# Two edits in a decoder-block kernel: weight casts and transposes held in another order ahead of the up projection, and the squares of x summed on VectorE instead of GpSimd

## The chip, the cores and the metric

The kernel runs on one core of one Trainium2 chip. The metric is the device time of one execution in microseconds (us), the median over the runs. The engines are TensorE (PE; its weight loads are listed apart as PEld), VectorE (DVE), ScalarE (ACT), GpSimd (POOL) and SyncE (SP); the last one here only issues DMAs.

## The reference, cut to what matters

One decoder layer over 512 tokens and 1024 features, in float32:

```
h  = RMSNorm(x) * g1
q, k, v, u_pool, u_gate = split(h @ w_in)
a  = differential attention(q, k, v)          8 heads, causal
p  = causal pooling with windows 2, 4, 8, 16, then w_pool
x1 = x + (sigmoid(g_A) * a + sigmoid(g_P) * p) @ w_out
h2 = RMSNorm(x1) * g2
x2 = x1 + relu(h2 @ w_up)^2 @ w_down
out = RMSNorm(x2) * gf
```

RMSNorm divides each token's row by the root of the mean of its squares. So the first norm needs the sum over all 1024 features of x squared, and the second needs the finished rows of x1.

## The kernel before

**Products.** Every large matrix is split in two reduced-precision float32 parts, hi (a rounded copy, made by ScalarE) and lo (the rest, a subtraction on VectorE, line 113). A product is three matmuls per tile: hi by hi, hi by lo and lo by hi. The tile of one matmul is 128 rows deep and 512 or 256 columns wide. Weights come from HBM through a few rotating raw buffers, are split, and their buffers are handed on when the last reader has finished.

**Order.** The program text gives each instruction its rank. A planner then fixes, before the run and from a time model of its own, the order of the instructions on each engine; at run time an engine works through its list and waits at the first instruction whose data are missing. The helper `after(later, earlier)` adds only an order between two instructions of one engine. Buffers of equal tag share memory: a tile waits until the tile before it under that tag has been read for the last time.

**The first stage** (lines 179 to 267). x arrives transposed, as eight tiles of 128 features by 512 tokens (`xprep`, line 179). For each of them ScalarE makes the hi part (line 184), VectorE the lo part (line 185), and ScalarE squares it (`xsquare`, line 190). In between come the splits of the weights of v (lines 112 and 113) and of the first q (`wq0`). TensorE starts at once on the first half of v and on q of head 0: 96 matmuls of lines 235 to 237 and 24 of `q0_step`. The squares of tile 0 go straight into the tile `ssx`; those of tiles 1 to 7 go into two alternating buffers, and GpSimd adds each one to `ssx` (line 197). When all are in, two small products with ones on TensorE (`pr`, line 251, and `pc`, line 256) add up the 128 rows, and `rsqrt` (line 200) makes from them the scales `rb` and `rcol`. `pr` and `pc` lie in two of the PSUM banks that the second half of v needs, and a third one is free only when the first half of v has been scaled with `rcol`; so three of the four accumulations of that half wait for this chain. Beside it VectorE works through a chain of small operations for the rotary angles (lines 287 to 321), which ends in a Sine on ScalarE (line 322), with a table load ahead of it and one behind it (line 323).

**The passage to the up projection** (lines 605 to 661). The output projection is computed in two halves of 512 features. The second half goes tile by tile over four tiles t of 128 tokens (line 625), each with eight k steps of three matmuls, of which the steps 6 and 7 need the last of four weight splits. Behind each tile: the sum with x (`x1_add`, line 587), the squares (line 561), the row scale (`row_scale`, lines 568 to 576: three small operations on ScalarE, two on VectorE), the scaled row tile h2 (line 636) and eight transposes on TensorE (line 644), whose results ScalarE and VectorE turn into the operands of the up projection (`forms_h2`, line 590). The up and down projections use a seven-product scheme over 2 by 2 blocks: the operands are the blocks A11, A12, A22 and the sums S1 to S4 (line 533). For the first quarter of the up projection (q = 0) the order is A11, A12, S1, S2, S3, A22, S4. A11 needs only token tiles 0 and 1. A12 and all after it need tiles 2 and 3 as well; S1 needs the parts that line 603 makes of tile 3. A product has four blocks (i, p) of twelve matmuls 256 wide.

**What holds the order there.** Tile t's first matmul stands behind the end of tile t-1 for every t from 1 (line 630). The transposes of tiles 0 and 1 stand behind the matmuls of tiles 1 and 2 (lines 631 to 633). In `up`, the transposes of tile 2 stand behind block (0,1) of A11 and those of tile 3 behind block (0,1) of A12 (lines 785 to 790). The weight casts for A11 (called b11) and A12 (called b21), two each, have no hold: they run as soon as a buffer is free. Those of S1 stand behind the row scale of tile 3 (line 729). The weights of S2 are made in place: when the splits of S1 have read their raw buffer, GpSimd issues a DMA that adds a further block to it (line 685).

Of the kernel before, what the change touches and what calls it, by code (L numbers as in the profile page):

```python
# [51 lines left out]
def block_kernel(ctx, tc, xT, x_tok, gains, pos, consts, w_in, w_v, w_pool, w_out, w_up, w_dn, out):  # L52
# [34 lines left out]
    def tmp(tag, name, shape=(P, S), dt=F32, bufs=2):  # L87
        return tp.tile(list(shape), dt, tag=tag, name=name, bufs=bufs)
# [82 lines left out]


    ssx = tmp("y", "ssx", bufs=1)
    vh = B16(2, F32R, "vh")
    vl = B16(3, F32R, "vl")
    rcol = cf.tile([P, NT, 2], F32, name="rcol")
# [12 lines left out]

    def xsquare(k):  # L190
        xt = gt0[:, k % 4, :]
        if k == 0:
            ins = A.activation(out=ssx, in_=xt, func=AF.Square)
        else:
            sq = tmp("sq", f"sq{k}")
            ins = A.activation(out=sq, in_=xt, func=AF.Square)
            G.tensor_tensor(out=ssx, in0=ssx, in1=sq, op=ALU.add)
        return ins

    def rsqrt(dst, src, t, n):  # L200

# [15 lines left out]
    for n in range(2):  # L217
        accs = [bank((0, 1, 2, 3, 4, 5, 6, 0)[4 * n + t], f"v{n}_{t}") for t in range(NT)]
        for kk in range(4):
            if n == 0:  # L220
                xprep(2 * kk)
            if n == 0 and kk == 0:
                raw, hi, lo = wv0
                nc.sync.dma_start(out=raw[:, 512:], in_=w_v[0, 0, :, 512:])
            else:
                raw, hi, lo = load_w(w_v[n, kk], f"v{n}_{kk}", 2 if n == 0 else 1)
            for k2 in range(2):
                if n == 0 and k2 == 1:
                    xprep(2 * kk + 1)
                sl = slice(k2 * 512, k2 * 512 + 512)  # L230
                split = split_w(raw, hi, lo, sl, eng=V)
                k = 2 * kk + k2
                for t in range(NT):
                    tsl = slice(t * P, t * P + P)
                    T.matmul(accs[t], lhsT=xh[:, k, tsl], rhs=hi[:, sl], start=k == 0, stop=False)
                    T.matmul(accs[t], lhsT=xh[:, k, tsl], rhs=lo[:, sl], start=False, stop=False)
                    T.matmul(accs[t], lhsT=xl[k][:, tsl], rhs=hi[:, sl], start=False, stop=k == NK - 1)
                if n == 0:
                    after(xsquare(k), split)
                    if k > 3:  # L240
                        q0_step(k - 4)
            if n == 0 and kk == 1:
                wq0 = load_w(w_in[0], "q0", 2)
            if n == 0 and 0 < kk < 3:
                i = kk - 1
                split_w(*wq0, slice(i * 512, i * 512 + 512), eng=V)
        if n == 0:
            for k in range(4, NK):
                q0_step(k)
            pr = bank(4, "pr")  # L250
            T.matmul(pr, lhsT=ones, rhs=ssx, start=True, stop=True)
            rsqrt(rb, pr, tmp("sq", "nt1"), D)
            A.mul(out=rb, in_=rb, mul=-0.5)
            pc = bank(5, "pc")
            for t in range(NT):
                T.matmul(pc[:, 2 * t : 2 * t + 2], lhsT=ssx[:, t * P : t * P + P], rhs=ones[:, 0:2], start=True, stop=True)
            rct = cf.tile([P, NT, 2], F32, name="rct")
            rsqrt(rcol, pc[:, 0:8].rearrange("p (a b) -> p a b", a=NT), rct, D)
            A.mul(out=rcol, in_=rcol, mul=-0.5)
        for t in range(NT):  # L260
            vd = [v_[:, 4 * n : 4 * n + 4, t * P : t * P + P] for v_ in (vh, f(vh), vl)]
            av = accs[t].rearrange("p (h d) -> p h d", h=4)
            A.activation(out=vd[0], in_=av, func=AF.Copy, scale=rcol[:, t, 0:1])
            V.scalar_tensor_tensor(
                out=vd[2], in0=av, scalar=rcol[:, t, 0:1], in1=vd[1],
                op0=ALU.mult, op1=ALU.subtract,
            )
# [357 lines left out]
    for t in range(NT):  # L625
        a_ = bank(4 + t, f"po1_{t}")
        for k in range(NK):
            m, end = mm_rows(a_, t, k, ws[k // 2], k == 0, k == NK - 1)
            if t and k == 0:
                after(m, state["po"])  # L630
        if 0 < t < 3:
            for b in range(2):
                after(state["h2T", t - 1, b], end)
        state["po"] = end
        x1_add(t, 1, a_)
        V.scalar_tensor_tensor(out=h2[:, t % 2], in0=x1[:, t, :], scalar=row_scale(t, 1), in1=g2b, op0=ALU.mult, op1=ALU.mult)
        pv = []
        for b in range(2):
            pt = bank((t % 2) * 2 + b, f"h2T{t}_{b}")
            for j in range(4):  # L640
                k = 4 * b + j
                if j == 1:
                    state["h2T", t, b] = state["h2T"]
                state["h2T"] = T.transpose(out=pt[:, j * P : j * P + P], in_=h2[:, t % 2, k * P : k * P + P], identity=ident)
            pv.append(pt.rearrange("p (j q) -> p j q", q=P))
        sl = slice((t % 2) * P, (t % 2) * P + P)
        if t > 1:

            A.copy(out=hw[:, 1, :, sl], in_=pv[0])
            V.tensor_tensor(out=hw[:, 0, :, sl], in0=pv[1], in1=hw[:, 1, :, sl], op=ALU.subtract)  # L650
            forms_h2((S1, S2), sl)
        if t == 3:
            forms_h2((S3,), slice(0, HS))
        for b in range(t // 2, 2):
            hi, lo = (gab[b][:, t // 2, i, :, sl] for i in range(2))
            A.copy(out=hi, in_=pv[b])
            part = V.tensor_tensor(out=lo, in0=pv[b], in1=f(hi), op=ALU.subtract)
            if t == 3:
                after(part, state[S3])
            if t < 2:  # L660
                A.copy(out=h2f[:, b, :, sl], in_=pv[b])
# [8 lines left out]
    def weights(src, q, nm, order):  # L670
# [16 lines left out]
        def parts(rs, b, hold=None, add=None):  # L687

            third = nparts[0] % 3 == 2
            nparts[0] += 1  # L690
            out_ = []
            for c in range(2):
                hi, lo = (
                    (bk if third else wp).tile([P, 1024], F32R, tag=t_ + "b" * third, name=f"{t_}_{nm}{b}_{q}_{c}", bufs=2 if third else 4)
                    for t_ in ("wh", "wl")
                )
                if add is None:
                    cast = split_w(rs[c], hi, lo, eng=V)
                else:

                    cast = A.copy(out=hi, in_=rs[c])
                    A.mul(out=lo, in_=f(hi), mul=-1.0)
                    G.dma_start(out=lo, in_=src[q, add, c], accum_op=ALU.add)
                if hold:
                    after(cast, hold)
                out_.append((hi, lo))
            return out_
# [52 lines left out]
    def up(q):  # L760
# [3 lines left out]
        def product(form, name, onto=None):  # L764
# [3 lines left out]
            for i in range(2):  # L768
                hi, lo = w[i]
                for p in range(2):  # L770
                    begin = None
                    a_ = pa[i][:, p * HS : p * HS + HS]
                    for k in range(4):
                        c = slice((p * 4 + k) * P, (p * 4 + k) * P + P)
                        m = T.matmul(a_, lhsT=hi[:, c], rhs=rh[:, k, :], start=p + k == 0 and onto is None, stop=False, skip_group_check=True)  # L775
                        first[-1] = first[-1] or m
                        begin = begin or m
                        T.matmul(a_, lhsT=hi[:, c], rhs=rl[:, k, :], start=False, stop=False, skip_group_check=True)  # L778
                    for k in range(4):
                        c = slice((p * 4 + k) * P, (p * 4 + k) * P + P)  # L780
                        m = T.matmul(a_, lhsT=lo[:, c], rhs=rh[:, k, :], start=False, stop=k == 3, skip_group_check=True)  # L781
                        if q == 0 and form == A12 and (i, p, k) == (1, 0, 0):
                            after(m, state["h2T"])
                    if q == 0:
                        if (form, i, p) == (A11, 0, 1):
                            for b in range(2):
                                after(state["h2T", 2, b], m)
                        elif (form, i, p) == (A12, 0, 1):
                            for b in range(2):
                                after(state["h2T", 3, b], m)  # L790
                        if form != A11 or i + p:
                            after(begin, state["um"])
                        state["um"] = m
# [226 lines left out]
```

## Time and profile before

| | |
|---|---|
| median of 3 runs | 676.74 us (676.6 to 678.25) |
| the profiled execution | 677.01 us, with a span of 675.1 us in the profile |
| TensorE busy | 664.3 us, 98% of the span |
| VectorE, ScalarE, GpSimd busy | 529.7, 461.6 and 122.3 us |
| granted TensorE clock, mean | 0.997 of full speed |

The difference between the profiled execution's time and its span, 1.9 us, lies outside the first and last instruction. A row of the timeline has start, duration, engine, line, operation, the tile written and the tiles read, the shape and a count if equal neighbours are merged; in brackets stands how long the engine had been idle and what released it. TensorE's matmuls overlap: a 512-wide one is listed with 0.39 us but the next one starts 0.227 us later, a 256-wide one with 0.28 and 0.12 us. So a stall is read from the starts.

### The profile page before, as it was taken

The numbers are of one execution on the slowest core, as the hardware profiler recorded it, in microseconds if no ns is written. First come the engines' busy times: TensorE is split into PE (matmuls) and PEld (weight loads), VectorE is DVE, ScalarE is ACT, GpSimd is POOL, SyncE is SP. The second block draws the span as 40 slices with busy tenths as digits, with TensorE's granted clock in tenths as the row PEclk, the third lists the DMA queues.
The fourth block names the chain that finished last, engine by engine and source line by source line (L and its number), as shares of the span: only waits on it lengthen the run. The fifth ranks groups of instructions, "written<-read, shape, count | busy, mean of one in ns | idle before, by whom it ended". The sixth has DMA issues, their size and how long they took to land.

```text
span 675.1 us, 9993 instructions
## 1 busy us (share of the span) xinstructions
PE 664.3 (98%) x3686; PEld 579.5 (86%) x3686; DVE 529.7 (78%) x879; ACT 461.6 (68%) x741; POOL 122.3 (18%) x137
## 2 busy tenths in 40 slices
PE   9999999999999999999999999999999999999995
PEld 7788888888888888888789988899889998899884
DVE  6955877799979986975578998657994599747995
ACT  8464587978887698883577875367743696356874
POOL 6201110132133212520202020202103021210120
PEclk9999999999999999999999999999999999999998
DMA  7526464335254364574964697776959579493863
GB/s 274 188 69 184 126 152 125 102 94 126 86 141 107 98 169 96 127 192 175 306 197 84 198 218 187 167 191 142 234 183 195 195 155 259 129 212 130 214 125 124
DMA packets 32880, 109.34 MB, mean 162 GB/s; under 512 B 4032, under 2 KB 4928, under 8 KB 32832
## 3 DMA queue, kind: packets, MB, share of 16 engines
q0 software_dynamic: 10656, 38.80, 32.2%
q1 hardware_dynamic: 21744, 69.38, 29.1%
q8 instruction: 29, 0.48, 0.3%
q10 hardware_dynamic: 432, 0.52, 0.2%
q14 instruction: 19, 0.16, 0.1%
HBM read 106.59 MB, written 2.10 MB: 161 GB/s over the span
## 4 chain that ended last, share of the span: by engine, by line
PE 95%; DVE 2%; issue 1%; DMA 1%; ACT 1%; SPq 0%; DVEq 0%
PE um L778 8%; PE um L775 8%; PE um L781 8%; PE dm L865 7%; PE dm L867 7%; PE dm L868 7%; PE o L417 2%; PE ga L132 2%; PE ga L131 2%; PE gp L135 2%; PE k L132 2%; PE gp L132 2%; PE k L131 2%; PE gp L131 2%; PE k L135 2%; PE ga L135 2%
## 5 line engine op out<-in xcount | busy, mean ns | idle before, releaser
L778 PE MATMUL um<-gss,wh_ut 128*128 128x256 f32 x192 | 48.2, 284 | 1.3 <-DVE gss L603 1.3
L867 PE MATMUL dm<-wh_dt,z 128*128 128x512 f32 (+1 forms) x128 | 49.5, 386 | 0.0
L868 PE MATMUL dm<-wl_dt,z 128*128 128x512 f32 (+1 forms) x128 | 49.4, 386 | 0.0
L865 PE MATMUL dm<-wh_dt,z 128*128 128x512 f32 (+1 forms) x128 | 49.3, 387 | 0.0
L775 PE MATMUL um<-gss,wh_ut 128*128 128x256 f32 x192 | 48.2, 283 | 0.0
L883 DVE TENSOR_TENSOR x<-x,dm 128x512 f32<-128x512 f32 x48 | 32.7, 682 | 18.3 <-PE dm L868 18.2
L400 ACT ACTIVATE p<-p,st 128x128 f32<-128x128 f32 (+3 forms) x64 | 35.7, 559 | 14.1 <-DVE st L396 13.8
L685 POOL DMA_DIRECT2D wga_dNone<-w_dn x16 | 14.2, 885 | 154.5 <-DVE wl_dt L113 154.5
L112 ACT CAST wh_ut<-wga_uNone 128x1024 fp32r<-128x1024 f32 x24 | 24.7, 1050 | 25.1 <-PE dm L867 19.5
L112 ACT CAST wh_ub<-wr_u 128x1024 fp32r<-128x1024 f32 x24 | 25.1, 1049 | 22.6 <-PE um L778 13.5
L778 PEld LDWEIGHTS um<-gss,wh_ut 128*128 128x128 f32 x192 | 36.9, 192 | 1.5 <-DVE gss L603 1.5
L867 PE MATMUL dm<-wh_db,z 128*128 128x512 f32 x96 | 37.2, 389 | 0.0
L868 PE MATMUL dm<-wl_db,z 128*128 128x512 f32 x96 | 37.2, 389 | 0.0
L685 POOL DMA_DIRECT2D wga_uNone<-w_up x18 | 15.6, 864 | 117.8 <-DVE wl_ut L113 93.2
L775 PEld LDWEIGHTS um<-gss,wh_ut 128*128 128x128 f32 x192 | 36.9, 192 | 0.0
L865 PE MATMUL dm<-wh_db,z 128*128 128x512 f32 x96 | 35.9, 389 | 0.0
L113 DVE TENSOR_TENSOR wl_ub<-wr_u,wh_ub 128x1024 fp32r<-128x1024 f32 x24 | 29.2, 1220 | 8.4 <-ACT wh_ub L112 8.3
L113 DVE TENSOR_TENSOR wl_ut<-wga_uNone,wh_ut 128x1024 fp32r<-128x1024 f32 x24 | 28.7, 1221 | 8.1 <-ACT wh_ut L112 8.0
L750 DVE TENSOR_TENSOR z<-rawz,z 128x1024 fp32r<-128x1024 f32 x28 | 33.6, 1219 | 1.3 <-ACT z L747 1.3
L747 ACT CAST z<-rawz 128x1024 fp32r<-128x1024 f32 x28 | 28.6, 1045 | 7.0 <-PE dm L868 3.2
L396 DVE CUSTOM_DVE_ANT_0 p<-s,mask 128x128 f32<-128x128 f32 (+3 forms) x64 | 30.3, 484 | 3.4 <-PE s L395 3.3
L112 ACT CAST wh_dt<-wga_dNone 128x1024 fp32r<-128x1024 f32 x24 | 24.9, 1049 | 11.8 <-issue 5.1
(324 smaller groups left out, 2221.1 us busy)
## 6 DMA issues: line engine op xcount, KB each, us to landing
wr_u<-w_up SPq DMA_DIRECT2D x24, 512.0 KB, 5.4
wr_d<-w_dn SPq DMA_DIRECT2D x24, 512.0 KB, 4.3
wga_uNone<-w_up POOLq DMA_DIRECT2D x18, 512.0 KB, 6.7
wga_dNone<-w_dn POOLq DMA_DIRECT2D x16, 512.0 KB, 5.5
wr_k<-w_in SPq DMA_DIRECT2D x8, 512.0 KB, 3.3
wr_ga<-w_in SPq DMA_DIRECT2D x8, 512.0 KB, 3.3
wr_gp<-w_in SPq DMA_DIRECT2D x8, 512.0 KB, 4.0
wl_ga<-w_in POOLq DMA_DIRECT2D x8, 512.0 KB, 5.4
```

The costliest lines, as they stand in the source:

```text
L112: ins = A.copy(out=hi[:, sl], in_=raw[:, sl])
L113: (eng or G).tensor_tensor(out=lo[:, sl], in0=raw[:, sl], in1=f(hi)[:, sl], op=ALU.subtract)
L131: T.matmul(acc, lhsT=hi[:, c], rhs=rh[:, k, :], start=k == 0, stop=False)
L132: T.matmul(acc, lhsT=hi[:, c], rhs=rl[k], start=False, stop=False)
L135: T.matmul(acc, lhsT=lo[:, c], rhs=rh[:, k, :], start=False, stop=k == NK - 1)
L400: A.activation(out=pr[:, c, :N], in_=pr[:, c, :N], func=AF.Exp, scale=-1.0, bias=st[:, c : c + 1], accum_out=st[:, 2 + c : 3 + c])
L775: m = T.matmul(a_, lhsT=hi[:, c], rhs=rh[:, k, :], start=p + k == 0 and onto is None, stop=False, skip_group_check=True)
L778: T.matmul(a_, lhsT=hi[:, c], rhs=rl[:, k, :], start=False, stop=False, skip_group_check=True)
L781: m = T.matmul(a_, lhsT=lo[:, c], rhs=rh[:, k, :], start=False, stop=k == 3, skip_group_check=True)
L865: m = T.matmul(a_, lhsT=zh, rhs=hi[:, sl], start=p == 0 and start, stop=False, skip_group_check=True)
L867: T.matmul(a_, lhsT=zl, rhs=hi[:, sl], start=False, stop=False, skip_group_check=True)
L868: end = T.matmul(a_, lhsT=zh, rhs=lo[:, sl], start=False, stop=p == 3, skip_group_check=True)
```

## The change

In the first stage, every squared tile now has its own slot in one tile `sqx` (eight slots of 512 columns, in the buffer that later holds the attention weights and then an operand of the up projection), GpSimd's seven additions are gone, and VectorE sums the eight slots in three additions (8 to 4, 4 to 2, 2 to 1), which the program text puts behind q of head 0 and ahead of `pr`. At the passage, four things change. Only tiles 2 and 3 of the output projection are still held behind the tile before, so tile 1 may start before tile 0 has ended. The transposes of tile 2 are held behind the matmuls of tile 3 (in place of block (0,1) of A11). The transposes of tile 3 are held behind the end of A11 (in place of block (0,1) of A12). And the second cast of b11 is held behind the row scale of tile 1, both casts of b21 behind that of tile 3.

```diff
     ssx = tmp("y", "ssx", bufs=1)
+    sqx = B16(4, F32, "sqx")
...
     def xsquare(k):
         xt = gt0[:, k % 4, :]
-        if k == 0:
-            ins = A.activation(out=ssx, in_=xt, func=AF.Square)
-        else:
-            sq = tmp("sq", f"sq{k}")
-            ins = A.activation(out=sq, in_=xt, func=AF.Square)
-            G.tensor_tensor(out=ssx, in0=ssx, in1=sq, op=ALU.add)
-        return ins
+        return A.activation(out=sqx[:, k, :], in_=xt, func=AF.Square)
+
+    def xsum():
+        for n in (4, 2):
+            V.tensor_tensor(out=sqx[:, 0:n], in0=sqx[:, 0:n], in1=sqx[:, n : 2 * n], op=ALU.add)
+        V.tensor_tensor(out=ssx, in0=sqx[:, 0], in1=sqx[:, 1], op=ALU.add)
...
                 q0_step(k)
+            xsum()
             pr = bank(4, "pr")
...
-            if t and k == 0:
+            if t > 1 and k == 0:
                 after(m, state["po"])
-        if 0 < t < 3:
+        if t:
             for b in range(2):
                 after(state["h2T", t - 1, b], end)
...
+        state["rows", t] = state["rows"]
...
+                if early and (b, c) in (("b11", 1), ("b21", 0), ("b21", 1)):
+                    after(cast, state["rows", 1 if b == "b11" else 3])
...
-                        if (form, i, p) == (A11, 0, 1):
-                            for b in range(2):
-                                after(state["h2T", 2, b], m)
-                        elif (form, i, p) == (A12, 0, 1):
+                        if (form, i, p) == (A11, 1, 1):
                             for b in range(2):
                                 after(state["h2T", 3, b], m)
```

## The prediction

> **What bounds the kernel now.** I read the page first, then the waits of TensorE and of its weight loads, then the timeline around each wait.
>
> ```profile
> span 675.1 us, 9993 instructions
> PE 664.3 (98%) x3686; PEld 579.5 (86%) x3686; DVE 529.7 (78%) x879; ACT 461.6 (68%) x741; POOL 122.3 (18%) x137
> ...
> PE 95%; DVE 2%; issue 1%; DMA 1%; ACT 1%; SPq 0%; DVEq 0%
> ```
>
> TensorE is busy for 98% of the span and makes 95% of the chain that ended last. The change removes no TensorE work, so it can give back only time in which TensorE stands still. The waits (engine, line, released by, us in total, times, longest), first of TensorE over the whole span, then of its weight loads in the stretch 0 to 60:
>
> ```profile
> PE um L778 <- DVE gss L603: 1.3, 1, 1.3
> PE v L237 <- DVE con L282: 0.6, 1, 0.6
> PE po L582 <- DVE wl_o L113: 0.4, 1, 0.4
> ...
> PEld v L237 <- DVE xlb L185: 1.0, 1, 1.0
> ```
>
> Apart from the start there are three. The first is laid to a one-element operation (L282) by TensorE's row; its weight load names the true releaser, the lo part of an x tile. The starts of the matmuls around them give what each costs:
>
> ```profile
> 21.02 0.39 PE L235 MATMUL v<-wh_v,xh 128*128 128x512 f32 x1
> 21.25 0.39 PE L236 MATMUL v<-wl_v,xh 128*128 128x512 f32 x1
> 22.22 0.50 PE L237 MATMUL v<-wh_v,xlb 128*128 128x512 f32 x1 [0.58 <-DVE con L282]
> 22.55 0.39 PE L235 MATMUL v<-wh_v,xh 128*128 128x512 f32 x1
> ...
> 330.30 0.39 PE L581 MATMUL po<-wh_o,vh 128*128 128x512 f32 x1
> 331.05 0.50 PE L582 MATMUL po<-wl_o,vh 128*128 128x512 f32 x1 [0.37 <-DVE wl_o L113]
> 331.39 0.39 PE L583 MATMUL po<-wh_o,vl 128*128 128x512 f32 x1
> ...
> 363.66 0.28 PE L775 MATMUL um<-gss,wh_ut 128*128 128x256 f32 x1
> 365.21 0.39 PE L778 MATMUL um<-gss,wh_ut 128*128 128x256 f32 x1 [1.27 <-DVE gss L603]
> 365.43 0.28 PE L775 MATMUL um<-gss,wh_ut 128*128 128x256 f32 x1
> 365.55 0.28 PE L778 MATMUL um<-gss,wh_ut 128*128 128x256 f32 x1
> ```
>
> Undisturbed, a 512-wide matmul starts 0.23 us after the one before (21.02 to 21.25) and a 256-wide one 0.12 (365.43 to 365.55). From 21.25 to 22.55 two of them took 1.30, so 0.84 is lost; from 330.30 to 331.39, 1.09 for two, so 0.63; from 363.66 to 365.43 two 256-wide ones took 1.77 in place of 2 x 0.12, so 1.53. Together 3.00 us: that is all the change can win. I take 0.3% of the median, 2.03 us, as what a measurement of this kernel can tell from no change.
>
> **First stage.** Two groups of the stretch 4 to 24 (behind the bar: busy us, mean ns of one), then rows of VectorE and of GpSimd:
>
> ```profile
> L113 DVE TENSOR_TENSOR wl_v<-wr_v,wh_v 128x512 fp32r<-128x512 f32 x8 | 8.7, 1105 | 1.3 <-ACT wh_v L112 1.3
> L185 DVE SCALAR_TENSOR_TENSOR xlb<-gx,con,xh 128x512 fp32r<-128x512 f32 x3 | 4.3, 1432 | 0.0
> ...
> 20.38 1.78 DVE L185 SCALAR_TENSOR_TENSOR xlb<-gx,con,xh 128x512 fp32r<-128x512 f32 x1
> 24.48 0.74 DVE L185 SCALAR_TENSOR_TENSOR xlb<-gx,con,xh 128x512 fp32r<-128x512 f32 x1
> 25.24 0.68 DVE L113 TENSOR_TENSOR wl_v<-wr_v,wh_v 128x512 fp32r<-128x512 f32 x1
> ...
> 18.61 3.00 POOL L197 TENSOR_TENSOR ssx<-ssx,sq 128x512 f32<-128x512 f32 x2 [1.03 <-ACT sq L196]
> ```
>
> The same instruction of VectorE takes 1.78 us while GpSimd adds (18.61 to 21.61) and 0.74 afterwards; the split takes 1105 ns on the mean and 0.68 afterwards. Without GpSimd these two groups alone give back 8 x (1.105 - 0.68) + 3 x (1.432 - 0.74) = 5.5 us of VectorE, and the lo part that TensorE awaited at 21.48 (21.25 + 0.23) would be ready at least 1.04 us earlier (1.78 less 0.74), hence before it is wanted. The Trainium skill, "SBUF — State Buffer", section "SBUF: two separate sides", says that a VectorE operation with two SBUF inputs and a GpSimd operation that reads SBUF lock each other out of a shared port pair for a whole instruction, while a DMA cannot slow either; the trace agrees (1.78 against 0.74), and by that rule the alternative that DMA traffic made VectorE slow falls away. Removed, then: 0.84 us of TensorE.
>
> Added are three additions on VectorE. 512 columns take 0.68 us (above), two operations of 1024 take 2.36 (the row at 354.56, below), so 1.18 each and 0.50 for the further 512. For 2048 columns no row exists; by that slope it is 1.18 + 1.00 = 2.2, at most 4 x 0.68 = 2.7. The sum is 2.2 + 1.2 + 0.7 = 4.1 us (4.6 at most), less than the 5.5 given back. The squares are now only written, and ScalarE's part of them is unchanged. GpSimd's queue holds nothing that gets later. What is queued behind the sum on VectorE is the chain of rotary angles, and who waits for that shows here:
>
> ```profile
> 33.03 0.18 DVE L321 TENSOR_SCALAR arg<-k__513 128x32 f32<-128x32 f32 x1
> ...
> 39.00 0.69 DVE L205 SCALAR_TENSOR_TENSOR nt<-pr,nt 128x512 f32<-128x512 f32 x1 [1.04 <-ACT nt L204]
> ...
> 33.69 1.02 PE L251 MATMUL pr<-ssx,onesr 128*128 128x512 f32 x2
> ...
> 40.94 0.39 PE L235 MATMUL v<-wh_v,xh 128*128 128x512 f32 x1
> ```
>
> The sum itself is wanted at 33.69, while the last lo part ends at 24.48 + 0.74 = 25.2 even with GpSimd in the way; 4.1 more is 29.3, so it is covered by 4 us. The angles end at 33.2, then come Sine, table load, casts, and the scale that frees the bank of `pr` at 39.69 (39.00 + 0.69). TensorE wants that bank at 40.94: 1.25 us of cover. As VectorE wins 5.5 and spends 4.1, the angles should not come later, and the cover shrinks only by the 0.84 that TensorE gains, to 0.41. I take nothing lost; bounds 0 and 2.9 (third rival).
>
> **Passage, tile 1 set free.** The split that TensorE waits for at 331.05 belongs to k steps 6 and 7 of tile 0. With tile 1 free, its steps 0 to 5, 18 matmuls, can stand in front of them, if the planner's model sees the wait. No row shows that: the gain lies between 0 and 0.63, and I take 0.30. Tile 0 may end up to 2 us later; its transposes stand 8 us behind the addition of its rows (next rows), so nothing waits.
>
> **Passage, holds and casts.**
>
> ```profile
> 332.51 0.69 DVE L587 TENSOR_TENSOR x<-po,x 128x512 f32<-128x512 f32 x1
> 350.63 0.69 DVE L587 TENSOR_TENSOR x<-po,x 128x512 f32<-128x512 f32 x1
> 353.36 1.29 DVE L636 SCALAR_TENSOR_TENSOR h<-x,st,rawz 128x1024 f32<-128x1024 f32 x1
> 354.56 2.36 DVE L113 TENSOR_TENSOR wl_ut<-wga_uNone,wh_ut 128x1024 fp32r<-128x1024 f32 x2
> 363.87 0.69 DVE L807 TENSOR_TENSOR rawz<-um,rawz 128x512 f32<-128x512 f32 x1 [0.95 <-PE um L781]
> 364.47 0.68 DVE L603 TENSOR_TENSOR gss<-hw,gss 128x512 fp32r<-128x512 f32 x1
> ...
> 341.17 1.03 PE L644 MATMUL h2T<-ident,h 128*128 128x128 f32 x8
> 357.05 0.28 PE L775 MATMUL um<-gab,wh_ub 128*128 128x256 f32 x1
> 359.92 1.04 PE L644 MATMUL h2T<-ident,h 128*128 128x128 f32 x8
> ...
> 352.78 1.98 ACT L112 CAST wh_ut<-wga_uNone 128x1024 fp32r<-128x1024 f32 x2
> 362.61 0.61 ACT L602 CAST gss<-hw 128x512 fp32r<-128x512 f32 x1
> 365.15 1.05 ACT L112 CAST wh_ut<-wga_uNone 128x1024 fp32r<-128x1024 f32 x1 [0.50 <-DMA wga_uNone<-w_up]
> ```
>
> Tile 3's rows are scaled by 354.65 (353.36 + 1.29), but its transposes stand at 359.92, where their hold ends. The new hold ends with A11, at 357.05: up to 2.9 us earlier. The lower bound comes from the planner's habit: tile 0's transposes stand at 341.17, 8.66 behind the row addition at 332.51, further than any wait demands. At that distance tile 3's would stand at 350.63 + 8.66 = 359.29, only 0.63 earlier. What S1 needs is line 603's lo part. Its input is cast at 362.61 and ready at 363.2, but on VectorE it stands behind the join of A12 (L807), which waits for TensorE to end A12 and starts at 363.87. So TensorE waits for an operation that waits for TensorE. With transposes 0.63 earlier the cast is ready at 362.6, 1.2 us before the lo part is wanted (363.66 + 0.12), and one addition of 0.68 fits if it now stands ahead of the join. If it still stands behind, the 1.53 remains. I give 80% to the first: 1.2 us.
>
> What pays for it: both b21 casts now stand behind tile 3's row scale, ahead of the two of S1, which start right behind it today, at 352.78. Two casts take 1.98, so those of b21 end at 354.8, and their splits, behind h2 (354.65), at 357.0. A12 starts at 357.05 on hi alone and wants lo eight matmuls later, at 358.0: covered by 1 us. S1's casts then end at 356.8 and its splits at 359.4, with five 0.6 us operations of tile 2 possibly in between at 362.4; S1 wants its lo weights at 364.6. Behind these splits GpSimd's DMA starts for S2: now the splits end at 356.9 (354.56 + 2.36) and the last block has landed at 365.15, 8.2 later. At 359.4 that is 367.6, at 362.4 it is 370.6, and two operations (2.2 us) follow; S2's second half wants them at 363.66 + 5.76 + 2.88 = 372.3 (48 and 24 matmuls at 0.12). So 0 to 0.5 us can come back there. I take 0, as the nearer end is the one without interleaving. The b11 cast moves by about 1 us and is wanted only in the second half of A11: nothing.
>
> **Sum.** 0.84 + 0.30 + 1.20 = 2.34 us. The profiled execution, 677.01 (span 675.1 and 1.9 around it), becomes 674.67; it lies 0.27 above the median of the runs, so I forecast 676.74 - 2.34 = 674.4.
>
> **The rivals.** (1) *The planner's order keeps the stalls at the passage.* For it: an order made from a model decides whether L603 passes L807 and whether tile 1 is used, and `after` edges alone don't enforce it. Then only 0.84 comes: 675.9. (2) *VectorE is slow for another reason than GpSimd.* Then 0.84 stays, the other 1.5 comes: 675.2. Against it speaks 1.78 beside 0.74. (3) *The sum delays the rotary angles.* If VectorE's idle stretches ahead of 21 merely grow and the 4.1 us come on top, L321 ends at 33.21 + 4.1 = 37.3, and the bank of `pr` is free 6.5 later (39.69 - 33.21), at 43.8, 2.9 us after it is wanted today (40.94). This decides from a delay of 0.41 us on. The 0.84 is lost in it too. Time: 679.6 if the passage gives nothing, 677.5 if it gives all of its 2.16 (0.63 + 1.53). The Trainium skill, "TensorE: Matmul & The Clock Gate", section "What's actually happening", lets the clock fall to half after an idle window of about 3.4 us; by an estimate from that page the price could rise by some 1.7 us, which no run here shows.
>
> **How the numbers follow.** Forecast 0.60 (673.7 to 675.4, five sixths of it more than 2.03 us faster), rival 1 0.20, rival 2 0.06, rival 3 0.14 (seven tenths of it slower by over 2.03). Faster: 0.50 and 0.02 from the edge of rival 2 make 0.52. Slower: 0.10. Same: 0.38. The range goes down to 673.6, where all of the 3.00 is won and a little more, and up to 677.2, which takes in rivals 1 and 2 and leaves out most of rival 3, some 0.12.
>
> **What would show it.** First stage: no L185 or L113 of 512 columns above 0.8 us, no wait for xlb, `pr` at about 32.85, the sum over before it. Passage: no wait of po for wl_o; tile 3's transposes before 359.9 counted from the same A11; L603 ahead of L807; no wait of um for gss. Wrong is the forecast if a wait of v on the scale appears near 40, if A12 or S2 waits for weights, or if the stall at S1 stays.

## The result and the profile after

The changed kernel takes 679.07 us (median of nine runs, 678.21 to 681.05), the kernel before beside it 676.74 (nine runs, 676.44 to 678.25). The ratio is 1.0030, with an interval of 1.0019 to 1.0042: slower by 2.3 us, where 2.3 us less was forecast. The range ended at 677.2.

The profiled execution of the changed kernel is its slowest, 681.05 us with a span of 678.9; where its extra 2 us come from is shown below. Of its page, the span, the busy times and the chain of waits (shares by engine):

```profile
span 678.9 us, 9984 instructions
...
PE 666.7 (98%) x3686; PEld 581.4 (86%) x3686; DVE 526.4 (78%) x882; ACT 461.1 (68%) x741; POOL 112.1 (17%) x130
...
PE 88%; DMA 5%; issue 3%; DVE 3%; ACT 1%; SPq 0%; POOLq 0%
```

TensorE's share of the chain fell from 95% to 88%, and DMA, 1% before, now has 5%. These shares say through what the chain runs, not what was lost. The waits of TensorE (three of its four rows; the fourth, ahead of the warm-up matmuls, is 1.1 us before and after):

```profile
PE um L782 <- DVE gss L604: 1.7, 2, 1.3
PE um L779 <- DVE rawz L808: 1.5, 2, 0.9
...
PE v L235 <- ACT wh_v L112: 0.6, 1, 0.6
```

The waits for `xlb` and for `wl_o` are gone, as forecast. The one for `gss` is there twice, and there is a new one, for the join of A22 (line 808; line numbers behind the first stage are one to four higher than before). In the timeline of TensorE:

```profile
5.50 2.08 PE L235 MATMUL v<-wh_v,xh 128*128 128x512 f32 x4 [0.58 <-ACT wh_v L112]
7.37 0.63 PE L236 MATMUL v<-wl_v,xh 128*128 128x512 f32 x1
7.80 0.63 PE L237 MATMUL v<-wh_v,xla 128*128 128x512 f32 x1
...
35.30 1.02 PE L252 MATMUL pr<-ssx,onesr 128*128 128x512 f32 x2
...
364.64 0.28 PE L779 MATMUL um<-gss,wh_ut 128*128 128x256 f32 x1
366.18 0.39 PE L782 MATMUL um<-gss,wh_ut 128*128 128x256 f32 x1 [1.27 <-DVE gss L604]
...
371.92 0.28 PE L779 MATMUL um<-gss,wh_ut 128*128 128x256 f32 x1
372.65 0.39 PE L782 MATMUL um<-gss,wh_ut 128*128 128x256 f32 x1 [0.44 <-DVE gss L604]
...
385.20 0.39 PE L779 MATMUL um<-gab,wh_ut 128*128 128x256 f32 x1 [0.64 <-DVE rawz L808]
...
389.20 0.39 PE L779 MATMUL um<-gab,wh_ut 128*128 128x256 f32 x1 [0.88 <-DVE rawz L808]
```

Three places explain the span. *Start:* the first matmuls start 0.43 us apart (7.37 to 7.80) instead of 0.23, and `pr` stands at 35.30, 1.61 later than before. *Tile 1:* at S1 the kernel is only 0.98 later (364.64 against 363.66), so the 0.63 of the `wl_o` wait have been won. *Passage:* the last row, A22's second half, stood at 385.41 before and is now 3.79 later. So 2.81 us were lost between S1 and A22, and 1.61 - 0.63 + 2.81 = 3.79 is the difference of the spans, 3.8.

The stall at S1 is unchanged (1.53). Counted in the same way, from the starts and with the 0.10 by which the matmul after a wait comes late, new are 0.71 at S2, 0.27 at S3 and 0.90 and 1.14 ahead of the two halves of A22 (0.16 at the second half before). What VectorE, GpSimd and ScalarE did in that stretch (the raw block of S2's weights is `wga_uNone`, its cast is `wh_ut`, its split `wl_ut`):

```profile
356.20 2.35 DVE L113 TENSOR_TENSOR wl_ub<-wr_u,wh_ub 128x1024 fp32r<-128x1024 f32 x2
358.48 1.22 DVE L113 TENSOR_TENSOR wl_ut<-wga_uNone,wh_ut 128x1024 fp32r<-128x1024 f32 x1
359.99 0.86 POOL L687 DMA_DIRECT2D wga_uNone<-w_up  x1 [23.89 <-DVE wl_ut L113]
360.81 1.22 DVE L113 TENSOR_TENSOR wl_ut<-wga_uNone,wh_ut 128x1024 fp32r<-128x1024 f32 x1
362.33 0.86 POOL L687 DMA_DIRECT2D wga_uNone<-w_up  x1 [1.47 <-DVE wl_ut L113]
364.84 0.69 DVE L808 TENSOR_TENSOR rawz<-um,rawz 128x512 f32<-128x512 f32 x1 [0.41 <-PE um L785]
365.44 0.68 DVE L604 TENSOR_TENSOR gss<-hw,gss 128x512 fp32r<-128x512 f32 x1
367.21 1.05 ACT L112 CAST wh_ut<-wga_uNone 128x1024 fp32r<-128x1024 f32 x1 [2.31 <-DMA wga_uNone<-w_up]
368.29 1.22 DVE L113 TENSOR_TENSOR wl_ut<-wga_uNone,wh_ut 128x1024 fp32r<-128x1024 f32 x1 [1.44 <-ACT wh_ut L112]
369.68 1.05 ACT L112 CAST wh_ut<-wga_uNone 128x1024 fp32r<-128x1024 f32 x1 [0.36 <-DMA wga_uNone<-w_up]
370.76 1.23 DVE L113 TENSOR_TENSOR wl_ut<-wga_uNone,wh_ut 128x1024 fp32r<-128x1024 f32 x1 [1.24 <-ACT wh_ut L112]
371.90 0.69 DVE L604 TENSOR_TENSOR gss<-hw,gss 128x512 fp32r<-128x512 f32 x1
...
388.46 0.69 DVE L808 TENSOR_TENSOR rawz<-um,rawz 128x512 f32<-128x512 f32 x1
```

It reads as a chain. The splits of b21, held back, now take VectorE at 356.20. So the splits of S1 come behind them, at 358.48 and 360.81. The DMAs for S2 wait for these, and start at 359.99 and 362.33 (356.08 and 357.21 before). Their blocks arrive for casts at 367.21 and 369.68. VectorE stands idle for 1.44 and 1.24, 2.68 together, and everything behind it in its queue is late: the lo part that S2 wants (371.90) and the joins ahead of A22. The lo part that S1 wants (365.44) still stands behind the join of A12 (364.84). This execution shows the wait at S2 rather small: the two blocks took 7.22 and 7.35 us from the DMA's issue to the cast here, and 7.9 to 8.0 in e2 and e13 below, which have the same hold and wait 1.3 us at S2.

Could VectorE make up for 2.68 us? The stretch 364 to 385, before and then after (columns: length, then busy us and count of PE, PEld, DVE, ACT and POOL, the granted clock, DMA share, GB/s):

```profile
364.00:385.00 21.00, 19.79 (x165) 19.79 (x166) 20.97 (x22) 17.01 (x22) 1.72 (x2) 1.00 0.56 151
```

```profile
364.00:385.00 21.00, 18.83 (x151) 18.02 (x149) 17.88 (x19) 16.70 (x22) 1.72 (x2) 1.00 0.71 168
```

Before, VectorE is busy for 20.97 of these 21 us. TensorE, "98% busy" over the span, has only 19.79 there, and what it lacks is the stall at S1. So VectorE had no slack in this stretch, and the first matmul of A22's second half followed its join almost at once (384.66 + 0.69 = 385.35, then 385.41):

```profile
384.66 0.69 DVE L807 TENSOR_TENSOR rawz<-um,rawz 128x512 f32<-128x512 f32 x1
...
385.41 0.39 PE L775 MATMUL um<-gab,wh_ut 128*128 128x256 f32 x1
```

The changed kernel has VectorE idle for 3.1 us of the stretch.

### The profile page after: what moved, and what is told of

Same layout as the page of the kernel before. It is cut to its first block, busy times and chain, and to the rows that moved or that the text cites. A ratio compares the mean times of both kernels' runs of the same rounds, so it can differ in the third digit from the quotient of the medians.

```text
span 678.9 us, 9984 instructions
## 1 busy us (share of the span) xinstructions
PE 666.7 (98%) x3686; PEld 581.4 (86%) x3686; DVE 526.4 (78%) x882; ACT 461.1 (68%) x741; POOL 112.1 (17%) x130
## 4 chain that ended last, share of the span: by engine, by line
PE 88%; DMA 5%; issue 3%; DVE 3%; ACT 1%; SPq 0%; POOLq 0%
PE dm L868 7%; PE dm L866 7%; PE dm L869 7%; PE um L779 6%; PE um L785 6%; PE um L782 6%; DMA wga_uNone<-w_up 4%; PE v L235 2%; PE v L236 2%; PE v L237 2%; PE o L418 2%; PE ga L132 2%; PE ga L131 2%; PE gp L135 2%; PE gp L132 2%
```

## The experiments

Theory D: the loss is made of S2's weights that land late and starve VectorE. Theory Q: in this stretch VectorE's queue is the bound, so that work put into it costs its length, and work taken out wins (in the later experiments, VectorE's and ScalarE's queues together). They don't exclude each other. All medians are of the kernel named, with the ratio to the kernel before beside it on the same chip.

| kernel | median us | ratio, interval |
|---|---|---|
| e1: the sum alone | 676.47 | 0.9995 (0.9987 to 1.0004) |
| e2: the passage alone | 680.00 | 1.0044 (1.0030 to 1.0058) |
| e3: the change without the hold on b21 | 676.22 | 0.9990 (0.9981 to 0.9999) |
| e4: the three cast holds alone | 680.85 | 1.0050 (1.0035 to 1.0064) |
| e5: two more operations on VectorE | 677.29 | 1.0006 (0.9998 to 1.0015) |
| e6: e3 with S4's weights held back | 675.74 | 0.9978 (0.9969 to 0.9986) |
| e7: before, with S4's weights held back | 678.46 | 1.0020 (1.0011 to 1.0029) |
| e8: e1 with ten warm-up matmuls | 676.44 | 0.9993 (0.9984 to 1.0002) |
| e9: before, S2's DMAs ordered later | 677.29 | 1.0001 (0.9990 to 1.0013) |
| e10: e3 with a lighter relief | 673.72 | 0.9953 (0.9939 to 0.9968) |
| e11: b21 held behind tile 2 | 676.77 | 1.0001 (0.9992 to 1.0010) |
| e12: before, S2's DMAs made late | 679.66 | 1.0032 (1.0021 to 1.0044) |
| e13: the change with the lighter relief | 676.90 | 0.9996 (0.9986 to 1.0006) |

**The parts: e1 to e4.** e1 takes the sum alone, e2 the passage alone; e3 is the change without the hold on b21, and e4 has the three cast holds alone:

```diff
 e1, from the kernel before (e2 undoes the same lines in the changed one):
+    sqx = B16(4, F32, "sqx")
-            G.tensor_tensor(out=ssx, in0=ssx, in1=sq, op=ALU.add)
+        return A.activation(out=sqx[:, k, :], in_=xt, func=AF.Square)
+            xsum()
 e3, from the changed kernel:
-                if early and (b, c) in (("b11", 1), ("b21", 0), ("b21", 1)):
+                if early and (b, c) in (("b11", 1),):
 e4, from the kernel before:
+        state["rows", t] = state["rows"]
+                if early and (b, c) in (("b11", 1), ("b21", 0), ("b21", 1)):
+                    after(cast, state["rows", 1 if b == "b11" else 3])
```

> Before, with the squares in eight tiles summed by VectorE, and nothing else. My theory: the sum wins the 0.84 us of the wait for the x tile's lo part and costs nothing, so 675.9 against 676.74 of before; no wait of v for xlb; the waits of po for wl_o (0.63 us) and of um for the S1 operand (1.53 us) stay as before. Rival: the sum is what made the changed kernel slow, through its first stage; then this kernel takes 678 or more and TensorE comes to the scale products later than before.

> The changed kernel with the squares added by GpSimd as before: all four edits at the passage, none in the first stage. Theory: the slowdown is the passage's, so this kernel is about 0.84 us slower than the changed one, 679.9; the wait for xlb is back, S1 waits 1.5 us, S2 0.7, A22 about 2 us. Rival (the first stage is to blame): 677 or less.

> The changed kernel without the hold on the two casts of A12's weights (b21); the hold of the second b11 cast, the freed tile 1 and the moved transposes stay. Theory: this hold moves S1's splits back, and with them the DMA that makes S2's weights, which lands 4 us late and pushes VectorE's queue into the joins; without it the waits at S2 and A22 (3.0 us) vanish: 676.0 from the changed kernel's 679.07, and 674.5 if the wait at S1 goes as well. Rival: the moved transposes are to blame; then S2 and A22 still wait and the time stays over 678.

> Before, with the three cast holds and nothing else. If the hold alone makes S2's weights late: 678 to 679, with waits at S2 and A22 as in the changed kernel. If it takes the hold together with the moved transposes, whose copies get between S1's splits on VectorE: S1's splits end about 2.3 us later than before (at 358 and 359.2), the DMA's blocks land near 366 and 367.5, in time for S2 at 371, and the kernel takes 676.3 to 677.2.

e1 was to win 0.84 and can't be told from the kernel before, though VectorE did what was forecast, as its timeline shows:

```profile
16.59 0.75 DVE L186 SCALAR_TENSOR_TENSOR xlb<-gx,con,xh 128x512 fp32r<-128x512 f32 x1
...
19.69 2.29 DVE L197 TENSOR_TENSOR sqx<-sqx 128x2048 f32<-128x2048 f32 x1
...
23.25 1.23 DVE L197 TENSOR_TENSOR sqx<-sqx 128x1024 f32<-128x1024 f32 x1
...
26.36 0.69 DVE L198 TENSOR_TENSOR ssx<-sqx 128x512 f32<-128x512 f32 x1
```

The lo part takes 0.75 and not 1.78, and the three additions make 4.2 us. e2 carries the whole loss, at the expected time (680.00 against 679.9): it lies in the passage. Between e2 and the changed kernel the sum makes 0.93, though e2's profile has only 0.31 of the wait for `xlb`. e3 takes the loss away again, so the hold on b21 is what costs. e4 shows that the three holds are enough without the other edits (that on b11, which e3 keeps, is among them), but it is slower than either forecast for it: the order of TensorE came out otherwise too, the largest wait is another one (2.15 us for ScalarE at 387.81, ahead of a first matmul of the down projection), and behind that wait TensorE ran at half pace for 3.5 us. How much of its loss is of that order and not of the hold stays open.

In e3 the moved transposes do what the prediction wanted of them: the lo part for S1 starts at 359.50, ahead of both joins of A12 (360.11 and 363.07). But e3 does not win what it should. It has no wait at S1 and none for `wl_o`, 2.16 us less than the kernel before. Its TensorE has these instead:

```profile
376.92 0.39 PE L779 MATMUL um<-gss,wh_ut 128*128 128x256 f32 x1 [0.61 <-ACT rawz L804]
...
380.37 0.39 PE L779 MATMUL um<-gab,wh_ut 128*128 128x256 f32 x1 [0.32 <-DVE rawz L808]
...
384.38 0.39 PE L779 MATMUL um<-gab,wh_ut 128*128 128x256 f32 x1 [0.87 <-DVE rawz L808]
```

By the starts they cost 0.78, 0.48 and 1.03, 2.29 together, and 2.59 with the 0.10 behind each that the 1.53 at S1 includes. The wait at S1 was not won but came back at S3 and A22. That speaks for theory Q, in a wider sense: in 364 to 385 e3 has VectorE busy for 19.15 of the 21 us and ScalarE for 18.85, and VectorE waited 1.02 and 1.07 for ScalarE's casts, so it isn't VectorE's queue alone.

**Work on VectorE: e5.**

```diff
+                if form == S1 and early:
+                    for _ in range(2):
+                        after(V.tensor_tensor(out=R[3].rearrange("p b c -> p (b c)"), in0=x1[:, 3, :], in1=x1[:, 3, :], op=ALU.subtract), state["lo"])
                 if form != A22:
                     adds = plus(ga, {S1: 3, S2: 2}[form])
```

> The kernel before with two subtractions of 1024 columns added on VectorE right behind S1's last weight split (some 1.2 us each, 2.4 in all); their result is not used. Nothing else moves: GpSimd's DMA issues for S2 stay at 356 to 357.3. Theory Q (VectorE's queue is full from tile 3's row scale to A22's second join, and A22's first matmul starts right behind the join): the 2.4 us push both joins back, TensorE waits there in new places, the wait of 1.5 at S1 may stay or grow, and the time is 2.0 to 2.5 above the kernel before: about 679. Rival D (the loss of the changed kernel comes from S2's weights, whose DMAs are issued 4 us later): no change here, 676.5 to 677. Rival S (there is slack behind S1 that absorbs it): also 676.5 to 677, with waits that grow at S1 and shrink again before A22.

It came out as rivals D and S had it, with a difference of 0.06% that can't be told from none. The timeline, VectorE, then GpSimd and two matmuls of the first stage:

```profile
355.93 1.22 DVE L732 TENSOR_TENSOR rawz<-x 128x1024 f32<-128x1024 f32 x1
...
357.66 1.22 DVE L732 TENSOR_TENSOR rawz<-x 128x1024 f32<-128x1024 f32 x1
...
362.95 0.69 DVE L810 TENSOR_TENSOR rawz<-um,rawz 128x512 f32<-128x512 f32 x1 [0.65 <-PE um L784]
...
384.19 0.69 DVE L810 TENSOR_TENSOR rawz<-um,rawz 128x512 f32<-128x512 f32 x1
...
18.74 3.34 POOL L197 TENSOR_TENSOR ssx<-ssx,sq 128x512 f32<-128x512 f32 x2 [1.27 <-ACT sq L196]
...
21.21 0.39 PE L236 MATMUL v<-wl_v,xh 128*128 128x512 f32 x1
21.43 0.39 PE L237 MATMUL v<-wh_v,xlb 128*128 128x512 f32 x1
```

The added 2.4 us filled gaps that VectorE has ahead of A12's last join, where it waits for TensorE: 0.65 is still idle there at 362.95. Up to that join nothing had moved: this run stands 0.92 earlier from the start on, and so does the join. A22's second join is 0.47 earlier than before, so it is late by only 0.45. Theory Q as I had written it was wrong in its place. VectorE is full from A12's last join on, not from tile 3's row scale on. So work of this length at 356 is not the cost by itself. (Here it stood behind S1's splits, in the changed kernel ahead of them.) That left D.

**The DMAs: e9, e11 and e12.** e9 and e12 leave the kernel before as it is and make S2's DMAs late; e11 holds b21 behind tile 2 and not tile 3.

```diff
 e9:
+                    if form == S1 and early:
+                        for i in adds:
+                            after(i, state["j1"])      # j1: first join of A12
 e12, ahead of the same two DMAs:
+                            g_ = ga[c][:, 0:1]
+                            after(V.tensor_scalar(out=g_, in0=g_, scalar1=1.0, scalar2=None, op0=ALU.mult), state["j1"])
 e11, from the changed kernel:
-                    after(cast, state["rows", 1 if b == "b11" else 3])
+                    after(cast, state["rows", 1 if b == "b11" else 2])
```

> The kernel before with one thing changed: the two DMA issues of S2's weights on GpSimd also wait for the first join of A12 on VectorE (it ends at 360.8), so that they start at about 360.8 and 362 instead of 356.1 and 357.2, as late as in the changed kernel (360.0 and 362.3). VectorE has the same work in the same order. Theory D (what the change costs at the passage is that S2's weights land late; VectorE, which has no idle time from A12's last join to A22's last, then stands idle 2 to 3 us ahead of S2's splits and delivers A22's joins that much later): casts of S2 at about 367.5 and 369.5, a wait at S2, waits ahead of A22, and 2.0 to 3.0 us more than the kernel before: 678.7 to 680. Rival Q (the cost is the work of VectorE itself that moved behind tile 3's row scale): no change, 676.5 to 677.3.

> The changed kernel with the b21 casts held behind tile 2's row scale instead of tile 3's: a smaller dose of the hold. Theory D: the casts run some 7 us earlier, their splits end ahead of tile 3's row scale, S2's DMA issues lie between those of the kernel without the hold (354.6, 355.7) and those of the changed kernel (360.0, 362.3), at about 355 to 358, S2's casts don't wait for long, and the time is that of the kernel without the hold or little more: 676.0 to 677.0. Rival Q2 (any hold on b21 costs by the order that the planner makes of it): 678 to 679.5 as in the changed kernel.

e9 moved nothing: its GpSimd issued at the same place (all of this run is 0.7 us later from the start on).

```profile
356.88 0.86 POOL L685 DMA_DIRECT2D wga_uNone<-w_up  x1 [22.02 <-DVE wl_ut L113]
```

The helper orders instructions of one engine, and the join is on another. So e9 says nothing on D; it shows what a kernel of equal order measures. e11 came out as theory D had it: the DMAs are issued at 355.79 and 358.12, neither S1 nor S2 waits, a join of A22 costs 0.51 + 0.10, and 1.26 + 0.10 are lost at 350.71, where TensorE is too early for an operand of tile 1. So it isn't any hold on b21 that costs the 2.3 us, but one that makes S1's splits, and with them the DMAs, late. That S1 doesn't wait in e11 is in part owed to the 1.36 us lost ahead of it.

> The kernel before with the two DMAs for S2's weights really made late: behind the first join of A12 VectorE multiplies one column of each of the two weight tiles by one, in place, and the DMAs add to these tiles, so that they can start only behind that (about 361.0 and 362, against 356.1 and 357.2 in the kernel before and 360.0 and 362.3 in the changed one). The earlier hold was only an order among GpSimd's own instructions and moved nothing. VectorE's other work is as before, with one split of S2 placed two operations later. Theory D (late landing of S2's weights starves VectorE in a stretch where it has no slack): S2's casts wait for their DMA until about 368 to 370, VectorE stands idle 1.5 to 3 us ahead of S2's splits, S2 waits, both joins of A22 come that much later and TensorE waits for them: 678.3 to 679.8. Rival Q (the cost is the work moved on VectorE, not the DMA): 676.3 to 677.3.

e12 gave 679.66, within theory D's range, but not by the path that was forecast. Its timeline:

```profile
361.12 1.76 POOL L685 DMA_DIRECT2D wga_uNone<-w_up  x2 [27.72 <-ACT hw L649]
366.60 1.05 ACT L112 CAST wh_ut<-wga_uNone 128x1024 fp32r<-128x1024 f32 x1 [1.66 <-DMA wga_uNone<-w_up]
367.68 1.23 DVE L113 TENSOR_TENSOR wl_ut<-wga_uNone,wh_ut 128x1024 fp32r<-128x1024 f32 x1 [2.08 <-ACT wh_ut L112]
369.19 1.05 ACT L112 CAST wh_ut<-wga_uNone 128x1024 fp32r<-128x1024 f32 x1 [0.50 <-DMA wga_uNone<-w_up]
...
381.37 0.39 PE L779 MATMUL um<-gss,wh_ut 128*128 128x256 f32 x1 [1.90 <-ACT rawz L807]
...
383.25 0.41 PE L779 MATMUL um<-gss,wh_ut 128*128 128x256 f32 x1
383.46 0.41 PE L782 MATMUL um<-gss,wh_ut 128*128 128x256 f32 x1
```

Two DMAs 5 us late and nothing else of weight: VectorE idle for 2.08, and 2.6 us more by the medians. So late landings alone cost time, and rival Q is out. But neither S2 nor A22's joins make TensorE wait here. ScalarE, which stood idle for 1.66 and 0.50 ahead of S2's casts and for 1.45 ahead of a cast behind them, was the first to be late, with a copy ahead of S3 (2.06 by the starts), and then TensorE ran some 3.4 us at half pace (0.21 for a 256-wide matmul instead of 0.12), which cost about 1.5 more. Without these 1.5 us, by estimate, the time would have been 678.2, just below D's range.

**The queue: e6, e7, e10 and e13.** If VectorE and ScalarE are the bound up to A22, the work that is not wanted before A22 should go behind it. e6 (and e7, on the kernel before) put both casts and splits of S4's weights behind A22's last copy and join. e10 (and e13, on the changed kernel) put back only the second half of them, and one sum and one split of the down projection's first weights:

```diff
 e6, from e3, and e7, from the kernel before:
+                if nm == "u" and q == 0 and b == "b22":
+                    after(cast, state["keep"])
+                    after(state["lo"], state["join"])
 e10, from e3, and e13, from the changed kernel:
+                if (nm, q, b, c) == ("u", 0, "b22", 1):
+                    after(cast, state["keep"])             # last copy ahead of A22
+                    after(state["lo"], state["joins"][2])  # A22's first join
+                if (nm, q, b, c) == ("d", 0, "b11", 0):
+                    after(state["lo"], state["joins"][3])  # A22's second join
...
+                if (nm, q, c) == ("d", 0, 0):
+                    after(sm, state["joins"][3])           # sm: ga[c] = r11[c] + al[c]
```

> The changed kernel without the hold on the b21 casts, and with the casts of S4's weights (b22, a later product) held behind the last copy that A22 needs on ScalarE, and their splits behind A22's last join on VectorE, so that the two full queues carry only what the passage wants. Theory Q: the waits at S3 and A22 (0.78, 0.47 and 1.03, 2.3 us in all) go, and nothing comes in their place: 673.7 to 674.5, below both kernels. Rival L: S4's weights are late in their turn and the waits reappear at S4 or at the first down projection: 675.8 to 676.5. Rival D (only S2's DMAs matter, and they are early already here): no change against the kernel without the hold, 676.2.

> The kernel before with only the holds on S4's weights (b22: casts behind the last copy that A22 needs, splits behind A22's last join). Theory Q: in the kernel before TensorE waits at S1 (1.5) for an order on VectorE, not for its load, and A22's joins cost nothing, so that nothing is won: 676.3 to 677.0, the wait at S1 still there; VectorE reaches A22's joins earlier and stands idle ahead of them. Rival: the wait at S1 shrinks as well, 675.2 to 675.8. Rival L: S4 waits for its weights, 677.5 to 678.5.

> The changed kernel without the hold on b21, and with less held back than in the earlier relief: of S4's weights only the second half (its cast behind the last copy that S3 needs, its split behind A22's first join), and of the down projection's first weights one sum and one split behind A22's second join. Theory Q (VectorE's and ScalarE's queues are what S3 and A22 wait for, once S1 doesn't wait any more): the waits of 0.78, 0.47 and 1.03 at S3 and A22 go, the down projection keeps its time since its weights are only 2.3 us later, and the time is 1.5 to 2.3 below the kernel without the hold: 673.9 to 674.8, below both kernels. Rival L (what is held back is wanted right behind): waits at the first down projection as in the earlier relief, 675.5 to 676.2.

> The changed kernel, its hold on b21 and all, with the light relief (second half of S4's weights, and one sum and one split of the down projection's first weights, placed behind A22's joins). Theory D and Q together: the relief takes the waits at S3 and ahead of A22 away (0.27, 0.91 and 1.14, 2.3 in all), while the 1.53 at S1 and the 0.71 at S2, which come of the late splits and landings, stay: 676.3 to 677.2. Rival (the relief alone repairs it): below 675. Rival (what is won at A22 is lost at the first down projection, since all runs later here): 678 to 679.

e10 is 3.1 us faster than the kernel before and 5.3 than the changed one, a little more than forecast. Its waits of TensorE, all of them:

```profile
PE warm L170 <- POOL eps L161: 1.1, 1, 1.1
```

Its two joins ahead of A22 and the stretch 364 to 385:

```profile
378.31 0.68 DVE L815 TENSOR_TENSOR rawz<-um,rawz 128x512 f32<-128x512 f32 x1
...
381.18 0.69 DVE L815 TENSOR_TENSOR rawz<-um,rawz 128x512 f32<-128x512 f32 x1
```

```profile
364.00:385.00 21.00, 21.00 (x177) 21.00 (x176) 19.34 (x19) 18.94 (x27) 0.86 (x1) 1.00 0.57 151
```

The joins end at 378.99 and 381.87, ahead of the matmuls that want them (379.24 and 382.12). TensorE is busy for all 21 us there, with 177 matmul records for 165 before. e13 keeps the hold: the waits at S3 and A22 go as in e10, and the two that come of the late splits and landings stay (2.2 us of idle time; by the starts 1.53 at S1 and 1.33 at S2, where 0.71 was expected):

```profile
PE um L789 <- DVE gss L604: 2.2, 2, 1.3
```

So the hold and the crowded queues are two causes that add up: 673.7 without either, 676.2 (queues alone) and 676.9 (hold alone), 679.1 with both. What the hold costs is its late splits (S1) and its late landings (S2); no run parts the two in the changed kernel. e6 held back too much: A22 didn't wait, but the first down projection lost 1.4 us waiting for its z parts; VectorE had stood idle for 2.26 us at 385.13, for a raw weight block that landed late. e7 shows the same loss without the gain, for in the kernel before A22 waited for only 0.16; in its profile 2.5 us go at the down projection and 0.65 at S3. Its 678.46 lies above the 676.3 to 677.0 of theory Q, and S4 itself did not wait.

**The start: e8.**

```diff
-    for _ in range(8):
+    for _ in range(10):
```

> The kernel before with x's squares in eight tiles summed by VectorE, and nothing of the passage, and ten in place of eight warm-up matmuls ahead of the first product (they compute nothing that is used). Theory W (the sum's gain of 0.84 at the start is eaten where TensorE runs its first products at half pace, starts 0.43 apart, for a time that differs between runs): two more warm-up matmuls bring the full pace to the first product, 675.7 to 676.1, and a narrower spread of the runs. Rival: the first product only starts later, or half pace stays as it is: 676.3 to 677.

No effect. The first product starts at 5.52 instead of 4.84 (e1) and still at half pace, until 7.17 instead of 7.47.

## Why the prediction was wrong, point by point

**What bounds the kernel.** I took TensorE's 98% of the whole span as the bound everywhere. In 364 to 385 VectorE has no slack either (20.97 of 21). The 3.00 us stand as what there was to win: e10, which has none of the three waits and none in their place, is 3.1 faster. But a wait of TensorE that goes is a gain only if the engine that TensorE waits for next has slack, and I did not look there. The 1.53 at S1 was such a wait: without it (e3) A22 and S3 asked for 2.59.

**First stage, 0.84.** The durations were right (0.75 in place of 1.78, 4.2 us of additions against 4.1 forecast, no wait for `xlb`). What it is worth is less sure. The wait of 0.84 in the profile of before is not in each execution of the same first stage: e5 has none (21.21 to 21.43, above), nor has e7, e12 has 0.05, e2 and e4 have 0.3, e9 has 0.85. Two things differ between them. In e5 and e7 VectorE has begun both of the splits that stand ahead of the lo part when GpSimd's last two additions begin (at 18.74 in e5, the splits at 17.94), and the splits take 1.28 us together; in the profile of before the additions begin at 18.61, ahead of the second split, and the two splits take 2.40. And in e12, where they take 2.39, TensorE comes later. By the medians the sum is worth 0.27 in e1, which can't be told from zero, and 0.93 between e2 and the changed kernel, two measurements apart in time; so 0.84 is neither confirmed nor refuted. The angles did come later (they end at 35.87 in e1 and at 33.21 before), against the forecast, and it cost nothing (rival 3, below).

**Tile 1 set free, 0.30.** The full 0.63 came: the wait is gone in the changed kernel, e3, e10 and e13. That the planner would use the freedom was a guess in the prediction.

**Holds and casts, 1.20.** The step that failed: "So 0 to 0.5 us can come back there. I take 0". The splits of S1 ended at 362.03 (360.81 + 1.22; 361.05 without the 0.98 by which the kernel is late there), on the side of the worst case that I had worked out (362.4), the DMA took 7.35 us to its cast (forecast 8.2), and S2 did wait for 0.71 (1.3 in e2 and e13), for the lo part of its operand that VectorE makes behind the late split. So far the working was right and the choice of its better end wrong. What the step left out weighs more: VectorE waits for the same blocks, in a stretch in which it has no slack, and with it the joins ahead of A22. That is 2.81 us at the passage in place of a gain of 1.20. The other half of the step fell too: line 604 stood behind the join as before (365.44 behind 364.84), so that S1's 1.53 stayed. I had given that 20%. Its cause was the hold, which the step had priced apart: without it (e3, e10) the lo part passes the joins as forecast.

**The rivals.** Rival 1 had the kept stall at S1, but not tile 1, and the price wrong, as it counted no new stall. Rival 3's 679.6 lies near the measured time by chance: the angles are late, but the planner put most of the chain for `pr` ahead of the Sine, and no matmul waits for its bank. Rival 2 fell with the durations. The prediction named the signs ("if A12 or S2 waits for weights, or if the stall at S1 stays"), and both came, S2 waiting behind the late weights' split and not for the weights themselves; no rival put a price on a wait at S2 or A22.

**The sum.** From e1 and the passage of the profiles: -0.27 - 0.63 + 2.81 = 1.9; measured 2.3. With the passage of e2's profile, where the blocks landed later and the loss is 3.44, it would be 2.5; the measured time lies between.

## What to carry to other kernels

Read the bound by stretch: a table of busy time over 20 us around the change would have shown VectorE at 20.97 of 21 where TensorE has 98% of the whole. Ahead of moving work, follow its last instruction to what it releases (here a buffer, then a DMA, then 7 us later a cast), and ask whether the engine behind that has slack. And a stall that is removed is worth only what the next engine in line leaves: here two waits of 2.2 us were removed (e3) for 0.5 us, and 3.1 us came only when work that nobody wanted yet had been taken out of the crowded queues (e10).

## What the runs showed of the hardware

At the start TensorE ran at half pace (0.43 us for a 512-wide matmul) for a time that differs between executions: to about 5.8 in the profile of before, 7.5 in e1, 10.8 in the changed kernel's, where 13 matmuls start from 5.50 to 10.80 and 24 did before. Eleven matmuls at 0.23 are 2.5 us, enough for the 2 us by which this execution lies above its median; no other execution of it has a profile to compare. The granted clock of the profile stands at 1.00 in both. In e12 and e4 the column does show it: 0.60 from 381.6 to 385.8, after TensorE had been idle for 2.06 us and had run about 1 us at full pace, and 0.51 from 388.6 to 392.1, after 2.31 us. The Trainium skill, "TensorE: Matmul & The Clock Gate", section "What's actually happening", has the clock at half by default and after an idle window of about 3.4 us, and at full after a busy one, with windows that run freely. The length of the half pace in e12, 3.4 us, agrees, while the idle time ahead of it was shorter than the window.
